# Weights rounded in an earlier up projection, rotary keys copied into the key tile, and a pool of its own for the first half of v

## The chip, the core and the metric

The kernel runs on one core of a Trainium2 chip. A core has five engines that work side by side: TensorE multiplies matrices (PE in the profile, PEld for its weight loads), VectorE (DVE) and ScalarE (ACT) work on elements, GpSimd (POOL) does the same more slowly, and SyncE (SP) issues most of the transfers between the chip's memory (DRAM) and the 128-partition on-chip memory (SBUF). The matrix products land in PSUM. The metric is the device time of one execution, in microseconds (us); less is better.

## The reference

One layer of a decoder on 1024 tokens of width 1024, all in float32. The parts around the change are these (the norms' gains, the mask and the two feed-forwards are shortened):

```python
x = x + 0.5 * swiglu(rmsnorm(x, ffn1_norm), ffn1_w_gu, ffn1_w_down)
h = rmsnorm(x, mix_norm); z = h @ w_in       # u, v, c_q, c_kv, k_rope, q_mem, gates
# A: spatial gating: chunks of 128 positions, 8 groups of 64 columns
y_a = u * (tril(sg_w) applied to layernorm(gelu(v)) + sg_b)
# B: latent attention, 8 heads of 64 + 32 (rotary) columns
q  = rmsnorm((rmsnorm(c_q) @ w_uq).reshape(S, 8, 96))       # then rope on the last 32
kv = (rmsnorm(c_kv) @ w_ukv).reshape(S, 8, 128)             # 64 of k, 64 of v
k  = rmsnorm(concat(kv[..., :64], broadcast(k_rope)))       # then rope on the last 32
y_b = causal_attention(q, k, kv[..., 64:])
# C: attention of 4 heads into 256 memory rows: kv = rmsnorm(mem) @ mem_w_kv
y_c = memory_attention(q_mem, mem)
x = x + (sum of sigmoid(gate_i) * (y_i @ w_branch_i)) @ w_out
x = x + 0.5 * swiglu(rmsnorm(x, ffn2_norm), ffn2_w_gu, ffn2_w_down)
```

## The kernel before

Every product is made of three passes in a rounded float32 format: an operand is split into a rounded part `hi` (ScalarE, line 134) and the rest `lo` (VectorE, line 137), and `mm3` (lines 153 to 155) multiplies hi by hi, hi by lo and lo by hi into the same PSUM bank. A weight must therefore be split before its product, or split once and stored to DRAM as a pair.

The stages follow each other: the first feed-forward's up projection (`up`, from unit 4 to unit 21, each unit 84 products), its down projection, the input projection with the gates, `token_rows` for v and the latents, then `mixer`: `qkv` (line 430), `sgu` (line 566) with the memory attention in it, the causal attention, and the merge. The second feed-forward closes.

Storing pairs early is already done for the memory's key and value weights: `weight_jobs` (line 670) makes eight jobs of two steps each. The first step takes a hi and a lo tile of the ring `wide` (five of each) and loads the raw weight into lo. The second step splits it and stores both to DRAM (`wkv`). `up` runs one step in each of its first 16 units. The queries' and keys' up-projection weights (`mla_w_uq`, `mla_w_ukv`) are loaded raw and split at the head of `qkv` (lines 436 and 437), into five pairs of `wide`; the spatial gating's weights `sg_w` are loaded, masked by GpSimd and split at the head of `sgu` (lines 570 to 577).

`qkv` goes over the 8 blocks of 128 tokens, two at a time. A block's q takes 18 products of 384 columns, its keys and values 12 products of 512. ScalarE copies them out and squares them into a single tile `sq`; VectorE sums the squares, finds the inverse root by 9 small steps, scales q and k (lines 482 to 488), GpSimd rotates the last 32 columns of q, and SyncE stores q, k and v to DRAM (`qd`, `kd`, `vd`). The tiles of q, k (two of each), v and sq lie in the pool `qkvp`.

When `qkv` has ended, the pool `qkvp` closes and `sgu` opens a pool of its own in the same space. It holds `v_hi` and `v_lo` for both halves of the tokens, so that the first of them can be written only when the last stores from `qkvp` have landed. `sgu` runs, in the order of its text: the split of v's first half, the first of two products for the memory's keys (48 products of 512 columns: `product` in `mem_kv`), layer norm and split of the second half, `mix(0)` (24 products of 256 columns and 16 transposes), the second product of `mem_kv` and 8 transposes, `mix(1)`, and the branch products among the steps of the memory attention. In the stages spoken of here the framework's scheduler orders each engine's queue by its own model of the times; only named stretches, and TensorE in `up`, stand as they are written. A queue runs in order: an instruction that waits holds all behind it.

The memory weights come back through `mem_weights` (line 770): of the four quarters for the keys three go to rooms outside the ring (two pairs of `h4`, one room of the pool `lt`) and one into `wide`; the four for the values go into `wide`, issued by ScalarE's queue.

Of the kernel before, what the change touches and what calls it, by code (L numbers as in the profile page):

```python
# [8 lines left out]
F32 = mybir.dt.float32  # L9
F32R = mybir.dt.float32r  # L10
# [6 lines left out]
P = 128  # L17
# [8 lines left out]
H = 8  # L26
# [23 lines left out]
class Kernel:  # L50
# [299 lines left out]
    def rotate(self, eng, pool, dst, src, tabs, shape):  # L350
# [8 lines left out]
        r = [pool.tile(shape, F32, name=f"rot{i}", bufs=1) for i in range(4)]  # L359
# [70 lines left out]
    def qkv(self, lat, asides):  # L430
# [4 lines left out]
        cq, krr, krs, eps = lat.cq, lat.krr, lat.krs, lat.eps  # L435
        wq = self.load(a["mla_w_uq"])
        wk = [self.load(a["mla_w_ukv"][g]) for g in range(2)]
        T = 2
        with tc.tile_pool(name="qkvp", bufs=2) as p:
            for i0 in range(0, NT, 2):  # L440
                q = p.tile([P, T, H, QK], F32, name="q")
                k = p.tile([P, T, H, QK], F32, name="k")
                v = p.tile([P, T, H, VD], F32, name="v", bufs=1)
                ss = self.stat("qk_ss", 2 * T * H).rearrange("p (a t h) -> p a t h", a=2, t=T)
                for t in range(T):
                    i = i0 + t
                    c = slice(i * P, i * P + P)
                    sq = p.tile([P, 2, 384], F32, name="sq", bufs=1)
# [13 lines left out]
                    sq = p.tile([P, 2, 384], F32, name="sq", bufs=1)  # L462
                    sq = sq.rearrange("p a b -> p (a b)")[:, :H * NOPE].rearrange("p (x d) -> p x d", x=H)
# [4 lines left out]
                    nc.vector.tensor_scalar(ss[:, 1, t], ss[:, 1, t], krs[:, i:i + 1], None, op0=ALU.add)  # L468
# [4 lines left out]
                v4 = var.rearrange("p (a t h) -> p a t h", a=2, t=T)  # L473
# [9 lines left out]
                self.rotate(nc.gpsimd, p, q[:, :, :, NOPE:], q[:, :, :, NOPE:], tabs, [P, T, H, half])  # L483
                nc.vector.tensor_tensor(
                    k[:, :, :, :NOPE], k[:, :, :, :NOPE], bk.to_broadcast([P, T, H, NOPE]), op=ALU.mult)
                mark = nc.vector.tensor_tensor(
                    k[:, :, :, NOPE:], krr[:, i0:i0 + T].unsqueeze(2).to_broadcast([P, T, H, ROPE]),
                    bk.to_broadcast([P, T, H, ROPE]), op=ALU.mult)
# [77 lines left out]
    def sgu(self, rows, p, sink):  # L566
        nc, a, tc = self.nc, self.a, self.tc
        v8 = lambda tag, dt=F32R: p.tile([P, 4, SGW], dt, name=tag, tag=tag, bufs=2)
        if True:
            ws = self.raw().rearrange("p (g t) -> p g t", g=SGG)  # L570
            nc.sync.dma_start(ws, a["sg_w"])
            nc.gpsimd.affine_select(
                out=ws, in_=ws, compare_op=ALU.is_ge, fill=0.0, base=0,
                pattern=[[0, SGG], [1, P]], channel_multiplier=-1,
            )
            whi, wlo = (x.rearrange("p (g t) -> p g t", g=SGG) for x in self.split_pair())
            self.split(whi, wlo, ws)
            vs, yt = {}, []

            def split(hf):  # L580
                vs[hf] = v8("v_hi"), v8("v_lo")
                for i, v in enumerate(rows[hf]):
                    self.v_mark = self.split(*(x[:, 2 * i:2 * i + 2] for x in vs[hf]), v)

            def mix(hf):
                if not yt:
                    yt.extend(self.split_pair() for _ in range(4))
                m, v = p.tile([P, 4, SGW], F32, name="u"), vs[hf]
                for g in range(SGG):
                    b = self.bank()[:, :4 * SGW // SGG].rearrange("p (c d) -> p c d", c=4)  # L590
                    cols = slice(g * SGW // SGG, (g + 1) * SGW // SGG)
                    self.mm3(b, (whi[:, g], wlo[:, g]), tuple(x[:, :, cols] for x in v), True, True)
                    nc.scalar.activation(m[:, :, cols], b, ACT.Identity, bias=self.sg_b[:, g:g + 1])
                for j in range(4):
# [3 lines left out]
                    for c in range(4):  # L598
                        nc.tensor.transpose(b[:, c * P:(c + 1) * P], m[:, c, j * P:(j + 1) * P], self.ident)
# [11 lines left out]
            rooms = [v8(n).rearrange("p (a b) w -> p a (b w)", a=2) for n in ("v_hi", "v_lo")]  # L611
# [8 lines left out]
            rooms = [v8(n, F32) for n in ("v_hi", "v_lo")]  # L620
# [34 lines left out]
    def rounded(self, src, dst, scaled=None):  # L655
# [3 lines left out]
        hi, lo = self.wide("whi"), self.wide("wlo")  # L659
        x = lo.bitcast(F32)  # L660
# [8 lines left out]

    def weight_jobs(self):  # L670

        self.wkv = self.dram.tile([2, 4, 2, P, D], F32, name="wkv")
        return [self.rounded(self.a["mem_w_kv"][g][:, 2 * c:2 * c + 2], self.wkv[g, c])
                for g in range(2) for c in range(4)]

# [66 lines left out]
    def mem_kv(self, mt, w):  # L742
# [11 lines left out]
        ps = product(w + self.mem_weights(0, [None], 3))  # L754
# [242 lines left out]
    def mixer(self, lat):  # L997
# [7 lines left out]
        def asides():  # L1005
# [4 lines left out]
            self.mem_w = self.mem_weights(0, [pair, pair, room])  # L1010
            yield

        with tc.tile_pool(name="lt", bufs=1) as p:
            room = lambda: tuple(p.tile([P, D], F32R, name=n) for n in ("whi2", "wlo2"))
            half = ROPE // 2
            for hf in range(2):
                t = slice(hf * 4, hf * 4 + 4)
                self.rotate(
                    nc.gpsimd, p, lat.krr[:, t], lat.kr[:, t], [x[:, t] for x in self.rope["k"]], [P, NT // 2, half])
            self.qkv(lat, asides())  # L1020
# [9 lines left out]
        with tc.tile_pool(name="sgu", bufs=1) as p:  # L1030
            yc = self.sgu(lat.v, p, sink_a)
# [1155 lines left out]
```

## Time and profile before

| | us |
|---|---|
| median of 3 runs (2200.07 to 2200.9) | 2200.32 |
| the profiled execution, its own time | 2199.52 |
| its span from the first to the last instruction | 2197.8 |
| busy in the span: TensorE, VectorE, ScalarE, GpSimd | 2166.6, 1581.6, 913.8, 270.2 |

All queries count time from the span's start. `qkv`'s first products of q start at 1060.14 us, `mem_kv`'s first at 1111.88 us, and the branch products of `sgu` at 1168.74 us. The views used below are: a table of stretches (busy time of each engine, mean granted TensorE clock, share of the transfer engines), the list of waits, the chain that ended last in order of time, groups of instructions by line and shape, and the timeline of an engine.

### The profile page before, as it was taken

What the parts mean: (1) busy time and instruction counts of PE and PEld (TensorE: products, weight loads), DVE (VectorE), ACT (ScalarE), POOL (GpSimd) and SP (SyncE); (2) the same over time, 40 slices, a digit from 0 to 9 for tenths busy, and PEclk for the clock granted to TensorE, in tenths of its full rate; (3) what the DMA queues carried; (4) which work ended last, traced back from release to release, by engine and by line L of the source; (5) the groups of instructions that cost most, each with busy time, mean ns of one, the idle gap of its engine ahead of it and who ended that gap; (6) DMA issues with size and microseconds to landing.
All of it is one profiled execution on the core that took longest, in us unless ns stands there. A gap on an engine that the chain in (4) does not pass through costs nothing.

```text
span 2197.8 us, 27491 instructions
## 1 busy us (share of the span) xinstructions
PE 2166.6 (99%) x10154; PEld 1807.2 (82%) x10154; DVE 1581.6 (72%) x2393; ACT 913.8 (42%) x1496; POOL 270.2 (12%) x274
## 2 busy tenths in 40 slices
PE   9999999999999999999979999999999999999999
PEld 5888888888887888888958889988888888888887
DVE  7976666679889656664966669885886666657884
ACT  5433333244445343433535459843433222234332
POOL 2011111100000000000221321140011111210000
PEclk9999999999999999999999999999999999999999
DMA  4253444484432455532566641094033233338443
GB/s 145 91 195 138 142 143 141 161 306 163 139 110 95 140 184 184 197 127 83 201 236 229 226 172 46 14 339 159 29 125 102 98 107 101 115 118 298 168 130 106
DMA packets 125367, 329.97 MB, mean 150 GB/s; under 512 B 14768, under 2 KB 23088, under 8 KB 125232
## 3 DMA queue, kind: packets, MB, share of 16 engines
q1 hardware_dynamic: 124080, 324.01, 42.3%
q10 hardware_dynamic: 1152, 4.19, 0.5%
q8 instruction: 80, 1.31, 0.2%
q14 instruction: 55, 0.45, 0.1%
HBM read 223.82 MB, written 104.33 MB: 149 GB/s over the span
## 4 chain that ended last, share of the span: by engine, by line
PE 89%; DVE 5%; ACT 2%; DMA 1%; issue 1%; POOL 1%; SPq 0%; ACTq 0%; POOLq 0%; DVEq 0%
PE one L153 15%; PE one L154 15%; PE one L155 15%; PE bank L153 12%; PE bank L154 12%; PE bank L155 12%; PE bank L937 1%; PE mm L153 1%; PE mm L154 1%; PE mm L155 1%; DMA qd<-q 1%; PE bank L952 1%; PE bank L953 1%; PE bank L423 1%; DVE wlo L142 1%
## 5 line engine op out<-in xcount | busy, mean ns | idle before, releaser
L141 ACT CAST whi<-x 128x1024 fp32r<-128x1024 f32 (+1 forms) x203 | 193.5, 955 | 444.8 <-PE one L154 167.9
L1347 DVE TENSOR_TENSOR t<-t,one 128x512 f32<-128x512 f32 x188 | 129.0, 686 | 213.6 <-PE one L155 213.5
L142 DVE TENSOR_TENSOR wlo<-x,whi 128x1024 fp32r<-128x1024 f32 (+1 forms) x203 | 246.9, 1218 | 35.1 <-ACT whi L141 25.8
L153 PE MATMUL bank<-h,whi 128*128 128x512 f32 x636 | 247.7, 390 | 0.0
L155 PE MATMUL bank<-h,wlo 128*128 128x512 f32 x636 | 247.5, 389 | 0.0
L154 PE MATMUL bank<-h,whi 128*128 128x512 f32 x636 | 247.4, 389 | 0.0
L153 PE MATMUL one<-h,whi 128*128 128x512 f32 x516 | 202.2, 392 | 0.0
L155 PE MATMUL one<-h,wlo 128*128 128x512 f32 x516 | 201.5, 391 | 0.0
L154 PE MATMUL one<-h,whi 128*128 128x512 f32 x516 | 201.4, 390 | 0.0
L153 PE MATMUL one<-w,whi 128*128 128x512 f32 x432 | 168.6, 390 | 0.2 <-DVE t L1347 0.2
L155 PE MATMUL one<-w,wlo 128*128 128x512 f32 x432 | 168.1, 389 | 0.0
L154 PE MATMUL one<-w,whi 128*128 128x512 f32 x432 | 168.1, 389 | 0.0
L137 DVE TENSOR_TENSOR wlo<-w,whi 128x1024 fp32r<-128x1024 f32 (+2 forms) x112 | 114.7, 1037 | 67.2 <-ACT whi L134 67.0
L134 ACT CAST whi<-w 128x1024 fp32r<-128x1024 f32 (+2 forms) x112 | 99.0, 902 | 148.5 <-PE one L154 63.9
L1927 POOL TENSOR_TENSOR raw<-raw 128x512 f32<-128x512 f32 x38 | 56.6, 1490 | 798.9 <-DVE raw L1782 712.2
L155 PEld LDWEIGHTS bank<-h,wlo 128*128 128x128 f32 x636 | 119.4, 188 | 24.9
L154 PEld LDWEIGHTS bank<-h,whi 128*128 128x128 f32 x636 | 119.4, 188 | 24.6
L153 PEld LDWEIGHTS bank<-h,whi 128*128 128x128 f32 x636 | 119.4, 188 | 24.6
L153 PE MATMUL bank<-whi 128*128 128x512 f32 x352 | 136.9, 389 | 0.0
L154 PE MATMUL bank<-wlo,whi 128*128 128x512 f32 x352 | 136.9, 389 | 0.0
L155 PE MATMUL bank<-whi,wlo 128*128 128x512 f32 x352 | 136.9, 389 | 0.0
L153 PEld LDWEIGHTS one<-h,whi 128*128 128x128 f32 x516 | 97.3, 189 | 20.2 <-issue 0.2
(394 smaller groups left out, 4922.8 us busy)
## 6 DMA issues: line engine op xcount, KB each, us to landing
x<-in_ffn_w_gu_dram SPq DMA_DIRECT2D x78, 512.0 KB, 4.8
w<-tdt SPq DMA_DIRECT2D x40, 512.0 KB, 4.4
gate<-raw SPq DMA_DIRECT2D x33, 512.0 KB, 2.8
tdb<-raw SPq DMA_DIRECT2D x64, 256.0 KB, 2.1
h<-in_ffn_w_down_dram SPq DMA_DIRECT2D x64, 256.0 KB, 5.9
w<-tdb SPq DMA_DIRECT2D x30, 512.0 KB, 4.6
tdt<-w SPq DMA_DIRECT2D x48, 256.0 KB, 2.1
x<-in_w_gate_dram SPq DMA_DIRECT2D x22, 512.0 KB, 6.9
```

The source lines that it names most:

```text
L134: i = self.nc.scalar.copy(hi, src)
L137: return (eng or self.nc.vector).tensor_tensor(lo, src, hi.bitcast(F32), op=ALU.subtract)
L141: self.nc.scalar.copy(hi, src)
L142: return lambda: self.nc.vector.tensor_tensor(lo, src, hi.bitcast(F32), op=ALU.subtract)
L153: i = mmul(out, s[0], m[0], start=first, stop=False, **kw)
L154: mmul(out, s[0], m[1], start=False, stop=False, **kw)
L155: self.last = mmul(out, s[1], m[0], start=False, stop=last, **kw)
L423: nc.tensor.transpose(b[:m, k * P:(k + 1) * P], s, self.ident)
L937: nc.tensor.transpose(b[:, at:at + P], prs[t][:, kk * P:(kk + 1) * P], self.ident)
L952: nc.tensor.matmul(o, w, pt[0], start=n == 0, stop=False)
L1347: return self.nc.vector.tensor_tensor(out, x, y, op=ALU.add)
L1927: sub = lambda d, x, y: (eng or nc.gpsimd).tensor_tensor(d, x, y, op=ALU.subtract)
```

## The change

Four things are changed.

1. `weight_jobs` makes six more jobs: three for `mla_w_uq`, two for `mla_w_ukv` and one for `sg_w` (its mask is applied in the job). They are stored as pairs in `wqs`, `wks` and `wss`. `up` takes a table of steps by unit: the eight old jobs keep their units 0 to 15, the six new ones take units 1 to 12, and a closing step runs ahead of an opening one. `qkv` and `sgu` load the pairs (`parts_of`) and split nothing. `up` here is that of the first feed-forward, from its unit 4 on.
2. GpSimd copies the rotated keys into the last 32 columns of each key tile before the block's products, so that one VectorE instruction scales the whole tile. The addition of the rotary keys' squares moves into a table `eps` that is made once, and two `scalar_tensor_tensor` take the place of five small steps for each pair of blocks.
3. The first half of `v_hi` and `v_lo` moves to a pool `pv` that is opened before `qkv`. The rotations' scratch moves to the ring `row`; `v` and `sq` move to the ring `raw` (three tiles), `mix`'s sums to the ring `h4`; the pool `lt` is gone.
4. The third quarter of the memory's key weights goes into `wide` as the fourth does.

```diff
@@ rotate
-        r = [pool.tile(shape, F32, name=f"rot{i}", bufs=1) for i in range(4)]
+        rows, n = [self.row() for _ in range(2)], shape[-2] * shape[-1] * (shape[1] if nd == 4 else 1)
+        dims = "p (t h f) -> p t h f" if nd == 4 else "p (t f) -> p t f"
+        r = [rows[i // 2][:, i % 2 * n:(i % 2 + 1) * n].rearrange(dims, f=half, t=shape[1]) for i in range(4)]
@@ qkv
-        wq = self.load(a["mla_w_uq"])
-        wk = [self.load(a["mla_w_ukv"][g]) for g in range(2)]
+        wq = [x for c in range(3) for x in self.parts_of(self.wqs[c], H * QK // 2)]
+        wk = [self.parts_of(self.wks[g], 512) for g in range(2)]
...
-                v = p.tile([P, T, H, VD], F32, name="v", bufs=1)
+                v = self.raw().rearrange("p (t h d) -> p t h d", t=T, h=H)
+                nc.gpsimd.tensor_copy(
+                    k[:, :, :, NOPE:], krr[:, i0:i0 + T].unsqueeze(2).to_broadcast([P, T, H, ROPE]))
...
-                    sq = p.tile([P, 2, 384], F32, name="sq", bufs=1)
+                    sq = self.raw()[:, :H * QK].rearrange("p (g x) -> p g x", g=2)
...
-                    nc.vector.tensor_scalar(ss[:, 1, t], ss[:, 1, t], krs[:, i:i + 1], None, op0=ALU.add)
...
-                for t in range(T):
-                    nc.vector.tensor_scalar(
-                        v4[:, 0, t], ss[:, 0, t], 1.0 / QK, eps[:, i0 + t:i0 + t + 1], op0=ALU.mult, op1=ALU.add)
-                nc.vector.tensor_scalar(v4[:, 1], ss[:, 1], 1.0 / QK, EPS, op0=ALU.mult, op1=ALU.add)
+                for n in range(2):
+                    nc.vector.scalar_tensor_tensor(
+                        var.rearrange("p (a t h) -> p a t h", a=2, t=T)[:, n], in0=ss[:, n], scalar=1.0 / QK,
+                        in1=eps[:, n, i0:i0 + T].unsqueeze(2).to_broadcast([P, T, H]), op0=ALU.mult, op1=ALU.add)
...
-                nc.vector.tensor_tensor(
-                    k[:, :, :, :NOPE], k[:, :, :, :NOPE], bk.to_broadcast([P, T, H, NOPE]), op=ALU.mult)
-                mark = nc.vector.tensor_tensor(
-                    k[:, :, :, NOPE:], krr[:, i0:i0 + T].unsqueeze(2).to_broadcast([P, T, H, ROPE]),
-                    bk.to_broadcast([P, T, H, ROPE]), op=ALU.mult)
+                mark = nc.vector.tensor_tensor(k, k, bk.to_broadcast([P, T, H, QK]), op=ALU.mult)
@@ sgu
-        v8 = lambda tag, dt=F32R: p.tile([P, 4, SGW], dt, name=tag, tag=tag, bufs=2)
+        v8 = lambda tag, hf, dt=F32R: (p if hf else self.pv).tile([P, 4, SGW], dt, name=tag)
...
-            self.split(whi, wlo, ws)
+            w = self.parts_of(self.wss, P, self.split_pair)
...
-                m, v = p.tile([P, 4, SGW], F32, name="u"), vs[hf]
+                m, v = [self.h4().rearrange("p a w -> p (a w)") for _ in range(2)], vs[hf]
...
@@ new, and weight_jobs
+    def parts_of(self, src, width, room=None):
+        n = src.shape[-1]
+        ts = [t[:, :n] for t in (room() if room else (self.wide("whi"), self.wide("wlo")))]
+        for t, x in zip(ts, src):
+            self.nc.sync.dma_start(t.bitcast(F32), x)
+        return [tuple(t[:, i:i + width] for t in ts) for i in range(0, n, width)]
...
+        small = [self.rounded(self.a["mla_w_uq"][:, 2 * c:2 * c + 2], self.wqs[c]) for c in range(3)]
+        small += [self.rounded(self.a["mla_w_ukv"][g], self.wks[g]) for g in range(2)]
+        small += [self.rounded(self.a["sg_w"], self.wss, causal)]
+        when = {}
+        for first, some in ((0, jobs), (1, small)):
+            for n, job in enumerate(some):
+                for f in range(2):
+                    at = when.setdefault(first + 2 * n + f, [])
+                    at.insert(0 if f else len(at), lambda job=job: next(job))
+        return when
@@ mem_kv, mixer
-        ps = product(w + self.mem_weights(0, [None], 3))
+        ps = product(w + self.mem_weights(0, [None] * 2, 2))
...
-            self.mem_w = self.mem_weights(0, [pair, pair, room])
+            self.mem_w = self.mem_weights(0, [pair, pair])
...
+        with tc.tile_pool(name="pv", bufs=1) as self.pv:
...
             self.qkv(lat, asides())
...
+            with tc.tile_pool(name="sgu", bufs=1) as p:
+                yc = self.sgu(lat.v, p, sink_a)
```

Where the new text puts the instructions is seen in the queues. **ScalarE, around the split of v's first half** (`v_hi_8866` before, `v_hi_8862` now; `h4_7863` and `h4_7909` are the first 256 rows of v). Before, it stands behind the last block's copies, the issues of the memory's value weights and the squares of the memory's keys (`t_8927`):

```order
L466 COPY v_8728<-mm_8801 128x512
L777 DMA whi_8954<-wkv_786 128x1024
L777 DMA wlo_8955<-wkv_786 128x1024
...
L777 DMA wlo_8967<-wkv_786 128x1024
L632 ACTIVATE t_8927<-mm_8876 128x512
...
L633 COPY h4_8925<-mm_8876 128x512
L134 CAST v_hi_8866<-h4_7863 128x1024
L134 CAST v_hi_8866<-h4_7864 128x1024
L593 ACTIVATE u_9034<-bank_9035,c_sg_b_3260 128x4x64
```

Now it stands among the copies of the first two blocks of `qkv`:

```order
L457 COPY q_8325<-bank_8375 128x384
L457 COPY q_8325<-bank_8387 128x384
L134 CAST v_hi_8862<-h4_7909 128x1024
L134 CAST v_hi_8862<-h4_7910 128x1024
L134 CAST x4_8125<-bank_8448 128x512
L134 CAST x4_8127<-bank_8455 128x512
L467 ACTIVATE raw_8369<-mm_8356 128x512
```

It has moved ahead by the whole of `qkv`, and the copies of the keys' latents (`x4_8125`) now stand behind it.

**TensorE, around the two products of `mem_kv`** (`mm_8876` and `mm_9121` or `mm_9122`; `bank_9035` and `bank_9036` are the first group of `mix(0)`). Before, the second product ends and `mix(0)` begins:

```order
L154 MATMUL mm_9121<-wlo_8967,h4_8452 128x512
L155 MATMUL mm_9121<-whi_8966,h4_8453 128x512
L153 MATMUL bank_9035<-v_hi_8866,x4_8862 128x256
L153 MATMUL bank_9040<-v_hi_8866,x4_8862 128x256
...
L154 MATMUL bank_9035<-v_lo_8867,x4_8862 128x256
```

Now the first product ends and `mix(0)` begins, with the second product behind its fourth group:

```order
L155 MATMUL mm_8876<-whi_8872,h4_8472 128x512
L153 MATMUL bank_9036<-v_hi_8862,x4_8858 128x256
L154 MATMUL bank_9036<-v_lo_8863,x4_8858 128x256
...
L155 MATMUL bank_9051<-v_hi_8862,x4_8859 128x256
L153 MATMUL mm_9122<-whi_8954,h4_8469 128x512
...
L153 MATMUL bank_9056<-v_hi_8862,x4_8858 128x256
```

`mix(0)` with its transposes has moved from behind the second product into it; behind it stay the 8 transposes and `mix(1)`.

More of the change, by code (lines that the diff above doesn't have):

```diff
@@ L567, in sgu @@
         nc, a, tc = self.nc, self.a, self.tc
[L568 removed]
+        v8 = lambda tag, hf, dt=F32R: (p if hf else self.pv).tile([P, 4, SGW], dt, name=tag)
         if True:
[L570 to L576, printed above, removed]
[L577 removed]
+            w = self.parts_of(self.wss, P, self.split_pair)
             vs, yt = {}, []
             def split(hf):
[L581 removed]
+                vs[hf] = v8("v_hi", hf), v8("v_lo", hf)
                 for i, v in enumerate(rows[hf]):
@@ L1941, in up @@
                     self.fetch(f)
-                for x in jobs[(f - first) // 2:][:1]:
-                    self.extra.append(lambda x=x: next(x))
+                self.extra += jobs.get(f - first, [])
                 self.unit(f)
```

58 lines of the change are left out of this document (33 added, 25 removed).

## The prediction

> **What bounds the kernel now.** First the page's busy times: TensorE is the engine that the span consists of, so only its holes and its slow clock are to be gained.
>
> ```profile
> PE 2166.6 (99%) x10154; PEld 1807.2 (82%) x10154; DVE 1581.6 (72%) x2393; ACT 913.8 (42%) x1496; POOL 270.2 (12%) x274
> ```
>
> Then the table of stretches, to find the holes (columns: length, busy us of PE, weight load, DVE, ACT and POOL with their counts, granted clock, share of the transfer engines, GB/s):
>
> ```profile
> 100.00:410.00 310.00, 310.00 (x1369) 256.78 (x1368) 215.29 (x264) 97.46 (x123) 45.61 (x32) 1.00 0.44 152
> 1075.00:1100.00 25.00, 25.00 (x133) 23.06 (x131) 22.63 (x50) 11.29 (x25) 11.14 (x12) 1.00 0.54 179
> 1100.00:1125.00 25.00, 20.70 (x93) 16.66 (x92) 21.08 (x45) 9.87 (x22) 6.66 (x7) 1.00 0.59 191
> 1125.00:1150.00 25.00, 17.09 (x71) 13.46 (x72) 7.43 (x36) 6.89 (x13) 4.42 (x6) 0.86 0.75 282
> 1150.00:1175.00 25.00, 19.27 (x107) 16.71 (x106) 20.79 (x31) 16.30 (x29) 0.00 (x0) 0.80 0.82 303
> ```
>
> The first two rows have no hole: the up projection, which gets new work, and the middle of `qkv`. The next three lack 4.30 + 7.91 + 5.73 = 17.9 us, and their clock of 0.86 and 0.80 costs 0.14 × 17.09 + 0.20 × 19.27 = 6.2 us more. All that this change can give back lies there, some 24 us, 1.1%. Who is waited for is in TensorE's list of waits from 1095 to 1170 us (total, times, longest):
>
> ```profile
> PE bank L153 <- ACT v_hi L134: 6.9, 1, 6.9
> PE mm L154 <- DMA wlo<-wkv: 2.5, 2, 1.7
> ...
> PE mm L153 <- ACT v L466: 1.7, 2, 1.2
> ...
> PE bank L153 <- ACT sq L454: 0.9, 1, 0.9
> ```
>
> Why ScalarE is late with `v_hi` is in the chain that ended last (start, us, what) and in ScalarE's timeline (start, us, line, operation, count, wait ahead of it):
>
> ```profile
> 1137.50 4.78 DMA qd<-q
> ```
>
> ```profile
> 1142.45 1.99 ACT L134 CAST v_hi<-h 128x1024 fp32r<-128x1024 f32 x2 [12.82 <-DMA qd<-q]
> ```
>
> The cast needs nothing of that store; it needs the room of `qkv`'s pool, which is free when the last store of q has landed at 1142.28. TensorE's own timeline shows both edges of the hole:
>
> ```profile
> 1137.31 0.39 PE L155 MATMUL mm<-whi,h 128*128 128x512 f32 x1
> 1144.55 1.20 PE L153 MATMUL bank<-v_hi,x 128*128 128x256 f32 x4 [6.85 <-ACT v_hi L134]
> ...
> 1147.19 0.41 PE L155 MATMUL bank<-v_hi,x 128*128 128x256 f32 x1
> 1147.40 0.41 PE L154 MATMUL bank<-v_lo,x 128*128 128x256 f32 x1
> ...
> 1168.74 0.48 PE L153 MATMUL bank<-x,whi 128*128 128x512 f32 x1
> ```
>
> After the hole the products start 0.21 apart, at a granted clock of 0.50.
>
> **Term A: product 2's end to the branch's start.** The hole goes, since the first half of `v_hi` has a room of its own and is cast among `qkv`'s first copies. From 1137.70 to 1168.74 are 31.0 us. What must still run between these two points, since the second half of v waits for the end of product 2 (its norm, its gate and then its casts follow it), is priced by the same instructions in the chain:
>
> ```profile
> 1143.53 2.36 DVE v_lo L137 x2
> ...
> 1153.19 1.05 ACT v_hi L134
> ...
> 1154.78 1.28 ACT L609
> 1156.28 1.03 ACT whi L134 x2
> 1157.30 0.58 ACT h L145
> ...
> 1158.92 0.52 ACT x L134
> ...
> 1160.02 0.90 ACT h L134
> ...
> 1161.44 0.39 ACT u L593
> ...
> 1168.55 0.44 PE bank L599 x4
> ```
>
> 0.5 for the last transposes of product 2's result, then 0.58 (`h`), 0.52 (`x`), 0.58 (`h`), 0.90 (cast of the values) and 2 × 1.05 (casts of v): 5.2. Then ScalarE's queue up to the first copy of `mix(1)`: 0.52 + 1.28 + 0.2 (the gap between the ends of L609 and the start of L134 behind it) + 2 × 1.03 + 0.52 = 4.6; the split's subtractions on VectorE, 2.36, lie beside it. Eight copies of `mix(1)` at 0.39: 3.1. The last two groups of transposes, 2 × 0.44: 0.9. Together 13.8 in place of 31.0.
>
> Against that, work of the 31.0 us has not gone, only moved ahead: 24 products of `mix(0)`, at full clock half of the 0.21 above, 2.6, and 16 transposes at 0.11 (0.44 for four), 1.8. It lengthens the stretch ahead by 4.4. Ten score products of the memory, 1.1, move behind the branch's start. A gives 31.0 − 13.8 − 4.4 − 1.1 = **11.7 us**. The cover that I count on is that ScalarE reaches the early casts in time; it has 11.29 of 25 us busy there.
>
> **Term B: the small waits ahead.** The 2.5 us for `wlo<-wkv` in the list of waits go: the value weights start when `qkv`'s last keys are scaled, and `mix(0)`'s first half (about 2 us) now runs in front of them. The waits in `qkv` come from VectorE, which has 22.63 of 25 us busy. Its groups between 1060 and 1130 us (busy, mean ns):
>
> ```profile
> L482 DVE TENSOR_TENSOR q<-q,rs_y 128x1536 f32<-128x1536 f32 x4 | 7.0, 1757 | 0.2
> L484 DVE TENSOR_TENSOR k<-k,rs_y 128x1024 f32<-128x1024 f32 x4 | 4.9, 1219 | 0.0
> L486 DVE TENSOR_TENSOR k<-h,rs_y 128x512 f32<-128x512 f32 x4 | 4.9, 1229 | 0.0
> L468 DVE TENSOR_SCALAR qk_ss<-qk_ss,krs 128x8 f32<-128x8 f32 x8 | 2.5, 309 | 0.2
> L464 ACT ACTIVATE sq<-mm 128x512 f32<-128x512 f32 x8 | 4.8, 598 | 14.4 <-DVE qk_ss L455 12.1 <-PE mm L155 2.3
> ```
>
> L484 and L486, 9.8 us, become one multiplication of 1536 columns, priced by L482: 4 × 1.757 = 7.0, so −2.8. L468 goes: −2.5. The first split's subtraction joins: +2.4. The scalar_tensor_tensor is in no trace here; between nothing and the 309 ns of L468 for each of its 8 instructions, in place of as many scalings, it is worth ±2.5 us of VectorE, and I take 0 (it replaces instructions of like size). The last row says that ScalarE's squares wait 12.1 us for VectorE to free `sq`, which is now in a ring of three. So I take TensorE's waits of 1.7 + 0.9 us for L466 and for the squares as gone, less 0.8 for the first blocks, where the copies of the latents now stand behind two casts of 1.05 (0.8, and not 2.1, since TensorE still has products of q to do beside them).
>
> B = 2.5 + 1.8 = **4.3 us** (bounds: 0, if VectorE's load is hardly less, and 5.1, without the 0.8).
>
> **Term C: the clock.** What the slow clock costs now is inside A's 31.0 us and goes with it. But a hole stays: of the 5.2 + 4.6 us ahead of the first copy of `mix(1)` TensorE fills about half with transposes and with the memory's scores, which leaves near 5 us. If the clock falls behind it as it does now, the 24 products of `mix(1)` take 24 × 0.21 = 5.1 us, in place of the 3.1 of the copies that A counts, and the transposes and first branch products some 0.5 more: **−2.5 us**. The ends are 0 (full clock) and −6.2 (all that the slow clock costs in the three stretches today).
>
> **The up projection: 0.** Six jobs add 6 casts (1.05 each, as for v) and 6 subtractions (2.36 for two), eight such jobs run there already. They would cost 6 × (1.05 + 1.18) = 13.4 us if nothing hid it. TensorE hides it: it is busy 310 of 310 us there while VectorE stands still for 95 and ScalarE for 212. The transfers have a share of 0.44.
>
> **GpSimd's copies: 0.** Four key copies with a broadcast have no row. From below 0, from above the nearest multiplication:
>
> ```profile
> L969 POOL COPY t<-a_inv 128x256 f32<-128x256 f32 x16 | 5.9, 399 | 30.9 <-DVE a_inv L966 30.9
> L360 POOL TENSOR_TENSOR rot<-q,rope_q 128x256 f32<-128x256 f32 x4 | 6.3, 1568 | 42.7 <-DVE q L482 42.7
> ```
>
> For 512 columns that is 0.8 (twice the first) to 3.1 each. I take the first, a copy like it; GpSimd waits 42.7 us in `qkv` ahead of L360, which hides even the second.
>
> **The sum.** 11.7 + 4.3 − 2.5 = 13.5 us off the profiled execution's own 2199.52: 2186.0. The median of the runs stands 0.8 above it: **2187 us**.
>
> **Rivals.** *1. The weights come late instead.* The third quarter of the memory's keys (two loads of 512 KB) and the branch's raw weights (1 MB) now load after `qkv`'s last products of q, into a stretch that is full:
>
> ```profile
> 1125.00:1130.00 5.00, 4.22 (x17) 3.19 (x18) 1.00 (x1) 2.06 (x4) 4.42 (x6) 1.00 1.04 411
> ```
>
> 2.1 MB at 411 GB/s are 5.1 us, which TensorE would wait at the c2 part of product 2 or at the branch: 2192, with a hole's clock up to 2195. Against it: half of `mix(0)` runs in front. 0.20.
>
> The Trainium skill, page "DMA: Bandwidth & Descriptors", section "Where 436 GB/s comes from", puts the HBM limit of one core at about 358 GB/s; by that the wait would be an estimated 5.9 us. The trace disagrees: 411 GB/s in the row above.
>
> *2. The up projection's transfer queue, the case that is slower.* SyncE's queue is in order; a job's load waits there for TensorE to free a `wide` tile (total, times, longest):
>
> ```profile
> SPq L661 <- PE one L155: 82.2, 7, 11.8
> ```
>
> Behind it stand the fetches of the next up weights. Their row among the page's transfers (KB, median us to landing), and one fetch and its first use, from the timelines of SyncE's queue and of VectorE:
>
> ```profile
> x<-in_ffn_w_gu_dram SPq DMA_DIRECT2D x78, 512.0 KB, 4.8
> ```
>
> ```profile
> 218.93 0.90 SPq L1303 DMA_DIRECT2D x<-in_ffn_w_gu_dram  x2
> 239.16 0.68 DVE L1320 TENSOR_TENSOR x<-x,x 128x512 f32<-128x512 f32 x1
> ```
>
> It is 20.2 us ahead (the sums at 220 cannot be its, since it takes 4.8 to land), so 15.4 us of lead. Now five tiles of `wide` are taken in each unit of a ring of five, where it was 4.5, and the waits grow. From a wait of 15.4 us on, TensorE stands. At 18 us it would lose (18 − 15.4) × 12 = 31 us, less the 13.5: 2218. Against it: the longest wait now is 11.8. 0.07.
>
> *3. The hole only moves.* The second half of v still waits for `qkv`'s last stores, and if product 2 ends ahead of them, the 6.85 us return there, with their clock: 13.5 − 6.9 and less, 2193 to 2200. Against it: product 2 now ends later by `mix(0)`, 4.4 us, and has the c2 wait ahead. 0.06.
>
> *4. No clock loss after a shorter hole.* In a stretch with 0.12 of 2 us busy the clock fell to 0.59:
>
> ```profile
> 1156.00:1158.00 2.00, 0.12 (x1) 0.12 (x1) 2.00 (x3) 1.99 (x6) 0.00 (x0) 0.59 0.51 209
> ```
>
> If the hole that is left came below that, the 2.5 of term C would not be lost: 2184.5. 0.05.
>
> By the Trainium skill, page "TensorE: Matmul & The Clock Gate", section "What's actually happening", half rate follows on at least one idle window of about 3.4 us; by that only a hole below 3.4 us, with the copies of `mix(1)` close behind, would give this. The row above speaks for less room: 0.59 in the course of a break of 1.9 us.
>
> **How the numbers follow.** The forecast has 0.62, the rivals 0.20, 0.07, 0.06 and 0.05. The range of the forecast alone, from the ends of B and C, is 2179 to 2194; to take in the first rival and most of the third, and a term A that is off by a third (3.9 us) on the fast side, it becomes 2177 to 2197. 0.2% is 4.4 us, about what a measurement of this kernel can tell from no change. Faster by more, below 2196: forecast, rivals 1 and 4, most of it, 0.86. Within: most of rival 3 and the tail of 1, 0.07. Slower: rival 2, 0.07.
>
> **What the new profile would show.** Right: ScalarE has no wait of 12.8 us for a store ahead of `v_hi`; TensorE's busy time from 1100 to 1125 is near 25; the branch starts near 1150 + the shift of `qkv` in place of 1168.74; one hole near 5 us ahead of `mix(1)`; the up projection is still at 310 of 310. Wrong: TensorE's waits for `wkv` loads or for `wide` of several us (rival 1), holes between 100 and 410 us with SyncE waits over 15 (rival 2), a wait for `qd<-q` ahead of the second casts (rival 3). What would break the forecast without any of them is a copy of the latents that stands far behind the early casts, so that `qkv` loses more than the 0.8.

## The result and the profile after

The changed kernel takes 2187.24 us (median of 4 runs, 2186.72 to 2188.78) against 2200.61 us (2200.07 to 2201.62): ratio 0.994, 95% interval 0.9923 to 0.9957, that is 9.5 to 16.9 us less. The forecast was 2187. The profiled execution is the slowest of the four (2188.78); its span is 2187.1 us, 10.7 less than before.

The page's busy times and the table of stretches, as before (us, PE, weight load, DVE, ACT, POOL with counts, clock, transfer share, GB/s):

```profile
PE 2163.5 (99%) x10154; PEld 1806.4 (83%) x10154; DVE 1570.0 (72%) x2374; ACT 912.4 (42%) x1491; POOL 271.8 (12%) x278
```

```profile
100.00:410.00 310.00, 310.00 (x1370) 256.69 (x1369) 214.47 (x272) 102.77 (x129) 45.58 (x33) 1.00 0.52 180
1075.00:1100.00 25.00, 24.08 (x124) 21.93 (x125) 22.66 (x43) 14.85 (x33) 11.24 (x13) 1.00 0.54 180
1100.00:1125.00 25.00, 25.00 (x125) 21.97 (x124) 20.49 (x41) 8.49 (x19) 11.44 (x13) 1.00 0.80 293
1125.00:1150.00 25.00, 17.08 (x91) 14.28 (x90) 17.27 (x51) 14.04 (x26) 1.36 (x2) 0.90 1.05 400
1150.00:1175.00 25.00, 24.83 (x136) 22.07 (x136) 13.85 (x25) 11.00 (x30) 3.44 (x2) 0.90 0.71 265
```

The first row is full with six more casts on ScalarE (x129 for x123): the up projection hides the jobs. From 1100 to 1125 us the holes are gone and from 1150 on nearly. The second row has lost 0.92 us that it did not lack before; the cause is at `qkv`'s start and is taken up with e2 and e9. Most of what is left lies between 1125 and 1150 us, with the transfer engines at a share of 1.05. TensorE's list of waits from 1000 to 1170 us (the last row is the wait at `qkv`'s start, the others lie between 1125 and 1152 us), and rows of its timeline at the two larger holes:

```profile
PE bank L153 <- ACT v_hi L134: 4.3, 1, 4.3
PE bank L153 <- ACT h L584: 2.3, 2, 2.1
PE bank L154 <- DVE v_lo L137: 1.5, 1, 1.5
PE bank L425 <- DVE x L137: 1.5, 1, 1.5
```

```profile
1129.56 0.39 PE L155 MATMUL mm<-whi,h 128*128 128x512 f32 x1
1132.09 0.39 PE L153 MATMUL bank<-v_hi,x 128*128 128x256 f32 x1 [2.13 <-ACT h L584]
...
1140.89 1.03 PE L425 MATMUL bank<-ident,h 128*128 128x128 f32 x8
1146.20 0.55 PE L153 MATMUL bank<-v_hi,x 128*128 128x256 f32 x1 [4.27 <-ACT v_hi L134]
...
1156.11 0.48 PE L153 MATMUL bank<-x,whi 128*128 128x512 f32 x1
```

The 6.85 us hole ahead of `mix(0)` is gone; the wait for `v_hi` that is listed now is that for the second half, ahead of `mix(1)`. The branch starts at 1156.11 and not at 1168.74. The first wait for L584 is new. The chain that ended last shows what is behind it:

```profile
1114.01 15.15 DMA vd<-raw
1129.24 0.33 ACTq L799
1129.61 0.60 ACT t L623
1130.21 0.48 ACT h L624
...
1131.66 0.38 ACT h L584
1132.09 0.39 PE bank L153
```

ScalarE's queue stands at the last load of the value weights (L799) until a store of v has landed, 15.15 us after its issue; the copies of product 1 (which ends at 1123.05) and of `mix(0)` stand behind that load. The load reads nothing of that store. In the program's order the two share a semaphore of the transfers, a counter that each of them raises when it has landed, and the load may be issued only when the store has raised it:

```
SP   L471 DMA vd_8278<-raw_8733 128x1024 [waits DMAHW4_49,Activation_49]
ACT  L799 DMA whi_8966<-wkv_786 128x1024 [waits DMAHW4_49,PE_49]
```

### The profile page after: what moved, and what is told of

The parts are those of the page before. It is cut to its first block, busy times and chain, and to the rows that moved or that the text cites. A ratio compares the mean times of both kernels' runs of the same rounds, so it can differ in the third digit from the quotient of the medians.

```text
span 2187.1 us, 27519 instructions
## 1 busy us (share of the span) xinstructions
PE 2163.5 (99%) x10154; PEld 1806.4 (83%) x10154; DVE 1570.0 (72%) x2374; ACT 912.4 (42%) x1491; POOL 271.8 (12%) x278
## 3 DMA queue, kind: packets, MB, share of 16 engines
q10 hardware_dynamic: 1152, 4.19, 0.5%
## 4 chain that ended last, share of the span: by engine, by line
PE 90%; DVE 5%; ACT 2%; DMA 1%; issue 1%; POOL 1%; SPq 0%; ACTq 0%; POOLq 0%; DVEq 0%
PE one L153 15%; PE one L154 15%; PE one L155 15%; PE bank L153 12%; PE bank L154 12%; PE bank L155 12%; PE bank L959 1%; PE mm L153 1%; PE mm L155 1%; PE mm L154 1%; PE bank L974 1%; PE bank L975 1%; DMA vd<-raw 1%; PE bank L425 1%; DVE wlo L142 1%
## 5 line engine op out<-in xcount | busy, mean ns | idle before, releaser
L142 DVE TENSOR_TENSOR wlo<-x,whi 128x1024 fp32r<-128x1024 f32 (+1 forms) x203 | 242.2, 1194 | 58.0 <-ACT whi L141 21.3
L155 PEld LDWEIGHTS one<-h,wlo 128*128 128x128 f32 x516 | 97.4, 189 | 20.4
```

Source lines behind the costliest of these rows:

```text
L142: return lambda: self.nc.vector.tensor_tensor(lo, src, hi.bitcast(F32), op=ALU.subtract)
L155: self.last = mmul(out, s[1], m[0], start=False, stop=last, **kw)
```

## The experiments

Each kernel was profiled and timed in five rounds (e1 and e9 eleven times) beside the kernel before on the same chip; e1 to e4, e5 to e8 and e9 to e12 ran on three different chips. A profile's start varies: the twelve transposes of `w` that stand ahead of `qkv` (L423 before, L425 after) begin at 1053.78 us before and 1055.22 after, and between 1053.7 and 1056.0 in all profiles, with and without the jobs. The shift arises in the first 100 us: the profiles in which TensorE gets through 359 or 360 products there have that mark at 1054.1 or earlier, those with 350 to 355 at 1054.9 or later. So the table counts from that mark, M. Columns: median and range of the runs in us, then from each profile M to the branch's first product, and from there to the end of the span.

| kernel | median (range) | M to branch | branch to end |
|---|---|---|---|
| before | 2200.61 (2200.07-2201.62) | 114.96 | 1029.06 |
| changed | 2187.24 (2186.72-2188.78) | 100.89 | 1030.99 |
| e1 both halves in the late pool | 2196.32 (2194.83-2198.19) | 111.92 | 1028.96 |
| e2 rounding taken back | 2185.42 (2183.90-2186.26) | 98.54 | 1029.55 |
| e3 keys taken back | 2189.94 (2185.07-2190.31) | 101.39 | 1031.13 |
| e4 last loads from SyncE | 2186.80 (2184.95-2188.93) | 98.14 | 1030.98 |
| e5 own pool alone | 2185.79 (2184.28-2187.16) | 98.91 | 1030.16 |
| e6 changed, again | 2187.11 (2186.70-2188.16) | 100.36 | 1030.92 |
| e7 two pools | 2185.19 (2184.73-2187.65) | 98.39 | 1030.98 |
| e8 two pools, SyncE | 2186.25 (2184.94-2188.81) | 98.11 | 1031.24 |
| e9 rounding alone | 2201.97 (2200.04-2203.56) | 117.00 | 1027.98 |
| e10 three jobs more | 2188.32 (2187.39-2189.32) | 100.80 | 1031.18 |
| e11 e5 and two pools | 2186.88 (2186.71-2189.08) | 101.84 | 1030.42 |
| e12 e8, queries later | 2190.68 (2188.78-2192.46) | 98.36 | 1034.58 |

**e6: the changed kernel again**, for the spread of a profile.

> The changed kernel once more, beside the others on this chip: 2187 +- 1.5 us, with the hole of some 2 us near 1130 us ahead of the second half of mix(0) and the one of some 4 us ahead of mix(1). If the time before qkv's first product (1061.6 in its first profile, 1060.1 before) is the start of an execution and not the six jobs, it differs between profiles of this same kernel by 1 us or more.

Both holes are there (1.8 and 4.3 us), and M is 1055.12, only 0.1 from the first profile, where 1 us or more was expected if the start alone decides. The shift is still not the jobs': e1, e7 and e10 have them and begin at 1053.7, e5 and e11 lack them and begin at 1055.0 and 1055.1. Single runs of one kernel spread over 2 to 5 us, so medians that lie 1 or 2 us apart tell little by themselves; the M columns and the waits say more.

**e1: is it the room?** The first half goes back into the pool that opens behind `qkv`; all else stays.

```diff
-        v8 = lambda tag, hf, dt=F32R: (p if hf else self.pv).tile([P, 4, SGW], dt, name=tag)
+        v8 = lambda tag, hf, dt=F32R: p.tile([P, 4, SGW], dt, name=f"{tag}{hf}")
```

> The changed kernel, but both halves of v_hi and v_lo lie in the pool that opens after qkv. Theory (the room of the first half carries the gain): mix(0) falls behind product 2 again, TensorE has a hole of 4 to 7 us ahead of it that ends with a cast of v_hi released by a store of q, and the branch starts 3 to 10 us later: 2190 to 2197 us. Rival (the gain is that the weights are rounded in advance and that VectorE has less to do): no hole comes back, 2187 +- 1.

9.1 to 9.2 us are lost (2196.32 against 2187.24 and 2187.11), and `mix(0)` stands behind product 2 again. TensorE's waits in this kernel:

```profile
PE mm L153 <- DMA whi<-wkv: 4.7, 1, 4.7
PE bank L153 <- ACT v_hi L134: 2.7, 1, 2.7
PE bank L154 <- DVE v_lo L137: 2.1, 2, 1.9
```

The loss is as the theory says, the hole not quite: 4.7 us of it come inside product 2, for weights that `mix(0)` no longer covers, and only 2.7 at `v_hi`, whose cast the profile puts down to a load of the branch's weights and not to a store of q. So the room gives two things at once, a cast that is done early and products that stand in front of a late transfer. That the loss is nearly what the prediction's terms A and C add up to is therefore in part luck: it is made up of other waits.

**e5: is the room enough?** The kernel before with the pool and what makes space for it (scratch, v and sq in the rings, mix's sums in `h4`, the third quarter in `wide`). Its core:

```diff
+        self.pvc = tc.tile_pool(name="pv", bufs=1)
+        self.pv = self.pvc.__enter__()
...
-                vs[hf] = v8("v_hi"), v8("v_lo")
+                vs[hf] = v8("v_hi", hf), v8("v_lo", hf)
...
-                    sq = p.tile([P, 2, 384], F32, name="sq", bufs=1)
+                    sq = self.raw()[:, :H * QK].rearrange("p (g x) -> p g x", g=2)
```

> The kernel before with only what gives the first half of v_hi and v_lo a pool of its own: the pool, the scratch, v, sq and mix's sums in the rings, the memory's third quarter in wide. Weights are rounded in qkv's place as before, keys are scaled in two steps, GpSimd copies nothing. Theory (the room carries the gain): 9 to 13 us faster than before, 2187 to 2191. Rival (the room gains only together with the rounded weights and the lighter VectorE): 2194 or more.

It gains 14.2 us by the medians (2199.98 on that chip, ratio 0.9935, 0.9922 to 0.9949), as much as the whole change or a little more. `qkv` has no wait of TensorE left either, though keys and steps are as before; the hole ahead of `mix(1)` is 6.9 us. So the pools and rings carry the gain, and with them the relief of the small waits.

**e2 and e9: the rounding in advance.** e2 takes five jobs out and loads and splits the weights ahead of `qkv` as before; e9 is the kernel before with the six jobs alone.

```diff
-        wq = [x for c in range(3) for x in self.parts_of(self.wqs[c], H * QK // 2)]
-        wk = [self.parts_of(self.wks[g], 512) for g in range(2)]
+        wq = self.load(a["mla_w_uq"])
+        wk = [self.load(a["mla_w_ukv"][g]) for g in range(2)]
```

> The changed kernel, but the query and key up weights are loaded as given and split ahead of qkv, as before; the five jobs in the up projection are gone. Theory (a job in the up projection costs nothing and gains nothing by itself): 2187 to 2190 us, the up projection's stretch 100 to 410 us has TensorE at 310 of 310 in both, and what is lost stands at the start of qkv. Rival (the weights carry the gain): 2195 or more. Second rival (the jobs cost the up projection time): faster than 2186.

> The kernel before with only the six jobs in the up projection and the loads of the rounded pairs; pools, keys and small steps as before. Theory (the rounding in advance is worth nothing in either direction): 2199 to 2201.5 us, TensorE busy 310 of 310 us from 100 to 410 us, the hole of some 7 us ahead of mix(0) stays. Rival (weights that need no split relieve qkv): 2196 or less. Second rival (the doubled loads of the weights or the jobs cost time): 2202 or more.

e2 is 1.7 to 1.8 us below the changed kernel and below its theory's band: all its five runs lie below the nine of the changed one, though not all on the same chip. e9 is at 1.0007 of before (0.9998 to 1.0016), which cannot be told from no change. Neither comes from the up projection, which is full in both; in e9:

```profile
100.00:410.00 310.00, 310.00 (x1370) 256.76 (x1368) 214.48 (x273) 102.80 (x130) 45.10 (x33) 1.00 0.53 181
```

What differs stands at `qkv`'s start. From 1060 to 1080 us TensorE is busy 20.00 us in the kernel before and in e2; these rows are of the changed kernel and of e9:

```profile
1060.00:1080.00 20.00, 18.51 (x97) 16.23 (x96) 17.86 (x56) 13.41 (x42) 4.95 (x16) 1.00 0.77 301
```

```profile
1060.00:1080.00 20.00, 18.93 (x102) 17.21 (x101) 13.57 (x51) 11.12 (x43) 2.20 (x8) 1.00 0.92 365
```

1.1 to 1.5 us are lost there. The pairs alone are not the reason, since e1 loads the same pairs and is busy 20.00 us. What e1 lacks is the early split of v. The two groups of transposes of the latents (L425), first in the changed kernel and then in e1:

```profile
1070.62 1.03 PE L425 MATMUL bank<-ident,h 128*128 128x128 f32 x8
...
1075.92 0.66 PE L425 MATMUL bank<-ident,h 128*128 128x128 f32 x4 [1.49 <-DVE x L137]
```

```profile
1069.11 1.03 PE L425 MATMUL bank<-ident,h 128*128 128x128 f32 x8
...
1072.90 0.60 PE L425 MATMUL bank<-ident,h 128*128 128x128 f32 x4
```

The second group waits for the split of what the first has transposed (`x`). The chain of the changed kernel shows what stands ahead of it on VectorE:

```profile
1072.83 2.43 DVE v_lo L137 x2
1075.26 0.61 DVE x L137
1075.92 0.66 PE bank L425 x4
```

It is the subtraction of v's early split, 2.43 us; on ScalarE the two casts of v stand ahead of the cast of `x` as well. In e1 that cast starts at 1070.08, in the changed kernel at 1073.90, though the first group is only 1.5 us later. So in the changed kernel this loss is the price of the early split. It needs the order that goes with the pairs as well: e2 and e5 have the early split without the pairs and are busy 20.00 us. Two other waits come up at the same place. e9, which has no early split, waits 1.1 us for `x`; there no product stands between the two groups. e6 waits 1.1 us for a load of a pair (`whi<-wks`) and 0.2 for `x`. Whether the doubled bytes of a pair cost anything by themselves was not tried.

e2 has no 2 us hole at 1130 us; there its order has two groups of `mix(0)` ahead of product 1.

**e3: the keys.** No copy on GpSimd, two multiplications.

```diff
-                nc.gpsimd.tensor_copy(
-                    k[:, :, :, NOPE:], krr[:, i0:i0 + T].unsqueeze(2).to_broadcast([P, T, H, ROPE]))
...
-                mark = nc.vector.tensor_tensor(k, k, bk.to_broadcast([P, T, H, QK]), op=ALU.mult)
+                nc.vector.tensor_tensor(
+                    k[:, :, :, :NOPE], k[:, :, :, :NOPE], bk.to_broadcast([P, T, H, NOPE]), op=ALU.mult)
+                mark = nc.vector.tensor_tensor(
+                    k[:, :, :, NOPE:], krr[:, i0:i0 + T].unsqueeze(2).to_broadcast([P, T, H, ROPE]),
+                    bk.to_broadcast([P, T, H, ROPE]), op=ALU.mult)
```

> The changed kernel without GpSimd's copy, with the two multiplications of 1024 and 512 columns for the keys; the rest stays. Theory: VectorE has 2.8 us more in qkv, where it is busy some 22 of 25 us, and 1 to 2.5 us of that come back as waits of TensorE: 2188 to 2190 us. Rival (VectorE's relief carries the gain): 2193 or more. Second rival (VectorE does not bound qkv now): 2187 +- 0.7.

The median lies in the theory's band, but its five runs fall into two groups (2185.1 and 2186.4; 2189.9 to 2190.3), and the trace shows no wait for VectorE in `qkv`; M to the branch is 0.5 to 1.0 longer. The way that the theory gave is not shown. VectorE does not bound `qkv` once `sq` is in a ring.

**e10: the jobs' cover.** Three more jobs in units 2 to 7.

```diff
+        self.wxs = self.dram.tile([3, 2, P, H * QK], F32, name="wxs")
+        more = [self.rounded(self.a["mla_w_uq"][:, 2 * c:2 * c + 2], self.wxs[c]) for c in range(3)]
...
-        for first, some in ((0, jobs), (1, small)):
+        for first, some in ((0, jobs), (1, small), (2, more)):
```

> The changed kernel with three more jobs in units 2 to 7 of the up projection that round the query up weights once more, into a room that nobody reads (work added, nothing left out). Theory (TensorE covers the jobs, and the lead of the weights' fetches is far from used up): 2187 +- 1.5 us and 310 of 310 us busy. Rival (the queue: seven takes of wide in a unit delay the fetches past their lead of some 15 us): holes in 100 to 410 us and 2190 or more.

SyncE's waits (total, times, longest) and the stretch of e10:

```profile
SPq L654 <- PE one L155: 24.8, 10, 11.8
```

```profile
100.00:410.00 310.00, 310.00 (x1369) 256.70 (x1368) 214.79 (x273) 105.05 (x132) 46.44 (x33) 1.00 0.56 191
```

The longest wait is 11.8 us, as before the change, and TensorE has no hole. With seventeen jobs the cover is not used up.

**e4, e7, e8: the holes that are left.** e4 issues the last quarter of the value weights from SyncE. e7 gives the key tiles of `qkv` a pool of their own, with the second half of `v_hi` in its room. e8 has both.

```diff
-                eng = self.nc.scalar if g else self.nc.sync
+                eng = self.nc.scalar if g and c < 3 else self.nc.sync
```

```diff
-        with tc.tile_pool(name="qkvp", bufs=2) as p:
+        with tc.tile_pool(name="qkvk", bufs=2) as pk, tc.tile_pool(name="qkvp", bufs=2) as p:
...
-                k = p.tile([P, T, H, QK], F32, name="k")
+                k = pk.tile([P, T, H, QK], F32, name="k")
...
-            with tc.tile_pool(name="sgu", bufs=1) as p:
+            with tc.tile_pool(name="sguh", bufs=1) as self.ph, tc.tile_pool(name="sgu", bufs=1) as p:
```

> The changed kernel, with the last quarter of the memory's value weights (two loads) issued by SyncE in place of ScalarE. Theory (the 2.1 us hole of TensorE at 1130 us is ScalarE's queue standing at the last of these loads, which a store of v releases, with the copies of product 1 and of mix(0) behind it): the hole goes, product 2 ends 2 us earlier, 1.4 to 2.1 us faster than the changed kernel, 2185 to 2186 us. Rival (the hole that comes next ends with the release of qkv's room and takes the time back): 2186.5 to 2187.5 us. Second rival (SyncE now stands at that load and its stores are late): 2188 or more.

> The changed kernel, with the key tiles of qkv in a pool apart from the query tiles and the second half of v_hi in the room of the key tiles, so that its cast waits for the last stores of k alone. Theory (what holds mix(1) is the room, released by the last store of q near 1142.8, and ScalarE's queue behind it): the second cast starts 3 us or more earlier and the branch 2 to 4 us earlier, 2183 to 2185 us. Rival (v_lo, whose room still waits for q, takes its place): 2186 to 2187.5 us.

> The two pools of e7 and the last quarter of the value weights from SyncE as in e4. Theory (two holes on the same path, each shortened at its own cause): 2 to 3 us below the changed kernel at the least, 2182 to 2184 us, below both kernels. Rival (the later of the two causes, the release by q's last store, sets the end in any case): as e7.

e4's hole at 1130 us is gone and M to the branch is 2.2 to 2.8 shorter, as forecast for ScalarE's queue; the median, 2186.80, shows 0.3 to 0.4 of it, within the spread of its runs. In e7 the second cast runs at 1136.53 and not at 1144.21, and the branch comes 2.0 to 2.5 earlier. Both together in e8 give no more than each. The timeline of ScalarE, the chain and TensorE's list of waits of e8 show what stands there instead:

```profile
1136.91 2.00 ACT L134 CAST v_hi<-h 128x1024 fp32r<-128x1024 f32 x2 [5.04 <-DMA t<-gate]
```

```profile
1128.86 7.95 DMA kd<-k
...
1136.87 5.21 DMA t<-gate
...
1142.09 2.35 DVE v_lo L137 x2
```

```profile
PE bank L153 <- issue: 5.6, 1, 5.6
```

The cast is 7.3 us earlier; VectorE's `v_lo` then stands, by the profile, until a gate row has landed. TensorE starts `mix(1)` at 1145.20, 1.0 us earlier than in the changed kernel. For its wait of 5.6 us the profile names nothing (issue). It ends 0.1 us after a step on VectorE (h L146) that stands directly behind `v_lo`, so VectorE's order may be what sets it; that is not shown.

**e11 and e12: past that.** e11 is e5 with the two pools. e12 is e8 with the queries' loads behind `mix(1)`:

```diff
-            late = self.mem_queries(1, iter([tuple(x[:, i] for x in rooms) for i in range(2)]))
             kv = next(kv)
-            queries = self.mem_queries(0, iter(lambda: self.split_pair(self.h4), None)) + late
             mix(1)
+            late = self.mem_queries(1, iter([tuple(x[:, i] for x in rooms) for i in range(2)]))
+            queries = self.mem_queries(0, iter(lambda: self.split_pair(self.h4), None)) + late
```

> e5 (the own pool alone) with the two pools of e7. In e5 the hole ahead of mix(1) is 6.9 us and ends with the cast of v_hi. Theory (that cast waits for the room that q's last store holds): the hole shrinks by 2 us or more, 2182.5 to 2184.5 us, below both kernels. Rival (as in e8, where the cast came 7 us earlier and the branch hardly: v_lo's room, the gate rows and VectorE's order take its place): 2185 to 2186.5 us.

> e8 with the loads of the memory's queries (8 loads of 512 KB) moved behind mix(1) in the order. Theory (in e8 mix(1) is held by transfers: the share of the transfer engines is 1.0 from 1118 to 1162 us, gate rows and the last stores of q land late): the branch starts 1 to 2.5 us earlier than in e8. Rival (the stores and gate rows are issued ahead of these loads anyway): the branch within 0.7 us of e8's. Second rival (the queries are then late for the memory's scores): slower than e8 by 1 us or more behind the branch's start.

In e11 the one hole of 6.9 us became three, and the branch is 2.9 later than in e5. Its list of waits:

```profile
PE bank L154 <- DMA t<-gate: 4.1, 1, 4.1
PE bank L153 <- DVE t L602: 2.9, 2, 2.0
PE bank L153 <- ACT v_hi L134: 2.8, 1, 2.8
```

In e12 the branch starts where it did in e8, and the memory's scores then wait for their queries: 3.3 us more behind the branch. Both of its rivals hold. The stores and gate rows are issued ahead of the queries in any case, so the queries do not hold them up; what would shorten the stretch further was not found. No kernel here is clearly faster than e2, e5 and e7, and of these only e2 is apart from the changed kernel in every run.

## Why the prediction was right

Term by term, in the profiles (before against after):

| step | forecast | measured |
|---|---|---|
| A: product 2's end to the branch | 31.0 to 13.8, with C 16.3 | 31.0 to 15.1 (1141.05 to 1156.11) |
| A: `mix(0)` and transposes moved ahead | +4.4 | +4.6 |
| A: scores moved behind the branch's start | +1.1 | +1.9 from the branch to the end, 1.2 of it ten scores |
| B: waits for the value weights | −2.5 | −2.5, and +2.1 at ScalarE's queue |
| B: waits in `qkv` | −1.8 | −1.1 (−2.6, and +1.5 for the early split) |
| small gaps, what is left over | none | −1.3 |
| up projection, GpSimd | 0 | 0 |
| sum | −13.5 | −12.1, and +1.4 at the profile's start: −10.7 |

The sum of the profile falls 2.8 us short of the forecast, half of it at the execution's start; the medians, which agree with it, differ by 13.4. That the median comes so close is partly luck: the changed kernel's profile is its slowest run, that of the kernel before lies below its other runs, and 1.3 us of the gain come from gaps that no term names.

Two statements of the prediction do not follow from its own terms. The ends of B and C give a sum of 5.5 to 16.8, so 2183.5 to 2194.8 and not 2179 to 2194; the low end needs the third of term A as well. And the terms put the branch's start at 1154.1, not near 1150; it was 1156.1, or 1154.7 without the later start.

- **Term A** was right in its cause. e1 takes 9.1 us away with the room, where A and C together said 11.7 − 2.5 = 9.2 (by other waits, as said there); e5 gets the gain without the other parts. The hole left ahead of `mix(1)` is 4.27 us and a wait of 1.5 for `v_lo`; near 5 were forecast. The 15.1 against 16.3 may be casts and products that overlapped a little more than in a plain sum; this was not followed up.
- **Term C** was right in kind, its size is measured only together with A: the clock fell behind the hole, and products of `mix(1)` start 0.21 apart. The table of stretches of the changed kernel:

```profile
1142.00:1144.00 2.00, 0.00 (x0) 0.00 (x0) 1.75 (x3) 2.00 (x4) 0.00 (x0) 1.00 1.02 402
1144.00:1146.00 2.00, 0.00 (x0) 0.00 (x0) 2.00 (x4) 2.00 (x4) 0.00 (x0) 0.70 1.03 418
...
1152.00:1154.00 2.00, 2.00 (x11) 2.00 (x11) 0.47 (x1) 1.61 (x4) 0.00 (x0) 0.50 1.02 399
1154.00:1156.00 2.00, 2.00 (x16) 2.00 (x15) 1.02 (x2) 0.78 (x2) 0.00 (x0) 0.74 1.03 402
```

  TensorE stops at 1141.92; a mean of 0.70 from 1144 to 1146 puts the fall at about 1144.8 (0.4 of the two microseconds at full clock), 2.9 us later, and 0.74 puts the return near 1155.0. The same reckoning for the kernel before (stop at 1137.70, 0.67 from 1142 to 1144) gives 5.0 us, so the time to the fall is not fixed; the 2.1 us hole at 1130 us left the clock at 1.00. The fourth rival, no loss of clock, did not come. The Trainium skill, page "TensorE: Matmul & The Clock Gate", section "What's actually happening", has half rate after at least one idle window of about 3.4 us; the 2.9 us of standstill here are a little less, the 5.0 before more.
- **Term B** was mis-sized: 4.3 us were forecast, and 2.5 − 2.1 + 1.1 = 1.5 came. The value weights' own wait went, but 2.1 us came back through the queue that issues them, which the prediction had not looked at. The relief of `qkv` came from the ring for `sq`, the reason that the prediction took from the squares' wait of 12.1 us: e9, which keeps one tile, keeps the waits of 0.9 and 1.8 us, and e5, which has the ring, has none. The move of v out of the pool, which e5 makes too, is not what helped: before the change the copies of v (L466) already followed the squares with no idle time ahead of them. VectorE's own saving, to which the prediction gave room beside it, did nothing that e3 can show. The early split cost 1.5 us in the profile, where 0.8 were taken: the prediction priced its casts on ScalarE, and its subtraction on VectorE (2.43) held the latents longer. Such a wait of the latents is what the prediction had named as able to break it.
- **The up projection** cost nothing (310 of 310, also in e10). Against the second rival the longest wait of SyncE for TensorE stayed at 11.8 us, and its waits for TensorE and for ScalarE's casts together, 160.3 us before, are 159.4.
- **GpSimd and VectorE's prices** held. The groups of the changed kernel:

```profile
L485 DVE TENSOR_TENSOR k<-k,rs_y 128x1536 f32<-128x1536 f32 x4 | 7.0, 1751 | 0.0
L446 POOL COPY k<-h 128x512 f32<-128x512 f32 x4 | 2.6, 664 | 0.2 <-DMA kd<-k 0.2
L476 DVE SCALAR_TENSOR_TENSOR qk_v<-qk_ss,eps 128x16 f32<-128x16 f32 x8 | 2.5, 322 | 0.1
```

  7.0 was said for the first and 0.8 each for the second (0.66). The third is 322 ns, a little over the 309 that was its upper end.
- **The first rival**, weights that come late, did come in another form (the 2.1 us, by way of the issuing queue), and in its own form once the cover was gone: 4.7 us in e1. **The third**, a hole that moves to the second half, was half true: 4.3 us stay there, but e7 and e8 show that the room is not the only thing that holds `mix(1)` there.

## What to carry to other kernels

A cast that needs nothing of a store can still wait for it, through the room. Giving the first consumer a room of its own, with the rings that made space for it, was worth the whole gain here, since it also put products in front of late transfers. Work that is moved ahead takes a place in its engine's queue: here it cost 1.5 us, because a split that TensorE needed soon stood behind it. Once the first wait is gone, look at what stands in the same queue: an engine that issues loads stops its own work at the first load that has to wait. In this stretch, with the transfer engines at a share above 1, taking away two of the waits together (e8) gave no more than taking away either.

## What was not expected of the hardware

- A load issued by ScalarE held up that engine's copies some 6 us beyond the end of product 1 (1123.05 to 1129.24), though the load needs nothing of what it waited for: it shares a semaphore with a store that took 15.15 us to land. From 1100 to 1145 us the median landing of loads and stores, tensor by tensor, is 4.5 to 10.3 us, against 3.8 to 8.7 before.
- The transfer engines keep 400 GB/s over 25 us (1125 to 1150 us, share 1.05). The Trainium skill, page "DMA: Bandwidth & Descriptors", section "Where 436 GB/s comes from", names about 358 GB/s as what binds such transfers for one core; the measurement is above it.
- The start of an execution moves everything behind it by up to 2.3 us (M at 1053.7 to 1056.0), more than most of the differences that these experiments asked about.
